# Two output projections from F32R to F16, with powers of two per channel that travel from the gated output into W_out

## The chip, the cores and the metric

The kernel runs on one core of one Trainium2 chip. The metric is the device time of one execution in microseconds (us), median over runs. The core has a matrix engine (PE, whose weight loads are listed apart as PEld), three elementwise engines (DVE, ACT, POOL) and a sequencer SP, on whose queue all DMAs of this kernel are issued. PE, DVE, ACT, POOL and SP each take their own instructions strictly in the order in which the program lists them and wait for each other through semaphores.

## The reference

Two layers over x of 1024 x 1024 f32; layer 0 mixes with forgetting attention (FoX, 16 heads of 64), layer 1 with native sparse attention (NSA, 4 groups of 4 heads).

```python
def reference(x, norm_g, fox_w_in, ..., nsa_w_out, final_g):
    for i in range(2):
        h = rmsnorm(x, norm_g[i])
        y = fox_mixer(h, ...) if i == 0 else nsa_mixer(h, ...)
        x = x + y
    return rmsnorm(x, final_g)

def fox_mixer(h, w_in, b_f, w_out):      # nsa_mixer ends in the same line
    q, k, v, f, z = split(h @ w_in)
    logits = q @ k.T * scale + c[:, None] - c[None, :]      # c: cumulated log-sigmoid of f
    o = softmax(causal(logits)) @ v
    return (o * silu(z)) @ w_out
```

What the change touches is the last line of both mixers: the gated output o*silu(z), 1024 tokens by 1024 channels, times W_out, 1024 by 1024.

## The kernel before

**Accuracy.** The results must be those of f32. A product A·B is made as three matmuls of half-precision-like parts, hi·hi + hi·lo + lo·hi (`mm3`, whose three lines are L225, L226 and L227; so every product in the profile shows those three lines). Parts are either F32R (an f32 tile rounded for the fast f32 path) or F16. The out-projections use F32R; layer 1's input projections use F16.

**Stages.** The span of 1461 us runs through: the opening (norm of x, transposes, first weights) to about 75 us; the body of FoX from there to about 510; the end of FoX with the first part of layer 0's out-projection to about 600, and the rest of that projection (`out_rest0`) to 639; NSA's projections and its compressed branch to about 957; NSA's selected and window attention to about 1387; and the rest of layer 1's out-projection (`out_rest`) with the final norm to the end.

**What sets the order.** Work is written as generators that yield their cost. `merge` takes a main generator (attention: `fox_main`, later NSA's) and a filler (`fox_fill`: the projections k, v, q, z of the next pairs of heads and then `out_start0`; in NSA `nsa_zs`: the z projections and then `out_start`) and emits so much filler per unit of main work. What comes out is one fixed order for each engine. So a matmul of the filler that waits holds up the attention's matmuls behind it, and the other way round.

**Pairs.** Heads come in pairs p = 0 to 7, a pair being 128 channels. `FoxDuo.finish` writes a pair's attention output into a tile `o` (L748; one buffer, used by one pair after the other), transposes it per half s of the tokens (s = 1, then 0), multiplies it on DVE by `vsc` and the gate silu(z) into the z tile (L758), and sends that f32 tile to `oF` in DRAM (L759). NSA's closing step does the same with DVE (L1642), POOL (the product by the gate, L1643) and a DMA. In the softmax L709 is DVE's score-and-maximum step, L718 ACT's exponential, L719 and L720 the F16 split of the probabilities, L721 their transposing DMA; in NSA the like are L1559 to L1566 and L242/L243.

**Out-projection.** W_out is copied from DRAM to DRAM at the start of each layer's filler (`wo_copy`, 16 DMAs of 512 KB), and loaded in halves of 512 rows by `load_wout`, which splits it in chunks of 128 x 512: ACT casts hi (L653), DVE or POOL in turn subtracts lo (L654). `out_start0` and `out_start` load 128-token tiles `of` from `oF` as their channels become ready, split them on ACT (L602, L1448) and DVE (L603, L1449), multiply, and add the product to the residual on DVE (L624, L1470). Pair 7, the last, also goes through `oF`. The split of a tile is emitted one half ahead of its matmuls:

```python
                if soon:
                    (load, split)[half](n + 1)
```

**Squares.** Powers of two that scale weights come from sums of squares: `early` and `late` load weight tiles `sq` and let ACT square them (L182), one step at certain points of the filler.

Of the kernel before, what the change touches and what calls it, by code (L numbers as in the profile page):

```python
# [8 lines left out]
F32 = mybir.dt.float32  # L9
# [12 lines left out]
P = 128  # L22
# [19 lines left out]
def tile_fox_nsa(ctx, tc, a, out):  # L42
# [160 lines left out]
    def gain_scale(gB):  # L203
# [12 lines left out]
        return e, b  # L216

# [130 lines left out]
    oF = dram.tile([D, S], F32, name="oF")  # L348
# [182 lines left out]
    def fox_z(p, w, halves=(1, 0)):  # L531
        zs = ready.setdefault(("zt", p), {})
        for half in halves:
            pt = ps_a(f"z{p}_{half}")
            yield from project(w, hT, half, pt)
            zs[half] = z = sb[0].tile([P, 512], F32, tag="z", bufs=4, name=f"z_{p}_{half}")
            silu2(z, pt)
            ready["z", p, half] = zs
# [4 lines left out]
                    + [(a["nsa_w_g"].rearrange("(k p) c -> p k c", p=P), 40)], 512, 1)  # L543
    first = []

    def fox_fill():
        for p in range(8):
# [12 lines left out]
            wo_copy(0, p)  # L560
# [5 lines left out]
            else:  # L566
                wq, wz = next_w(), next_w()
                yield from fox_q(p, wq, (1,))
                yield from fox_z(p, wz, (1,))
                rows0 = load_wout(hp, 0, 1)  # L570
# [3 lines left out]
                yield from fox_z(p, wz, (0,))  # L574
                yield from out_start0(load_wout(hp, 0, 0))
# [3 lines left out]
    def out_start0(rows1):  # L579
# [11 lines left out]
        def load(n):  # L591
# [4 lines left out]
            pend[n] = wp.tile([P, KC, P], F32, tag="wst", bufs=1, name=f"of0_{t}_{k}"), *out_parts(f"0_{t}_{k}")  # L596
            dma(pend[n][0][:, k:stop, :], oF[k * P:stop * P, t * P:(t + 1) * P].rearrange("(k p) t -> p k t", p=P))

        def split(n):
            _, k, stop = parts[n]  # L600
            of, oh, ol = (x[:, k:stop, :] for x in pend[n])
            A.copy(oh, of)  # L602
            V.tensor_tensor(ol, of, f(oh), OP.subtract)  # L603
# [4 lines left out]
        split(0)  # L608
        for n, (t, k0, stop) in enumerate(parts):
# [4 lines left out]
            for half in range(2):  # L614
                if soon:
                    (load, split)[half](n + 1)
# [7 lines left out]
                V.tensor_tensor(xs0[t][:, cs], pt, xs0[t][:, cs], OP.add)  # L624
            if more and not soon:
# [15 lines left out]

    def load_wout(pool, i, half):

        hi, lo = (pool.tile([P, 4, D], F32R, tag=f"h{half}{x}", name=f"wo{i}_{half}_{x}") for x in range(2))
        for k in range(4):
            r = 4 * (1 - half) + k
            dma(f(lo[:, k, :]), wD[i][r * P:(r + 1) * P, :])
        yield 0
        for k in range(4):
            for c in range(2):  # L650
                yield 400 if i else 200
                cs = slice(c * 512, c * 512 + 512)
                A.copy(hi[:, k, cs], f(lo[:, k, cs]))  # L653
                (V if c else G).tensor_tensor(lo[:, k, cs], f(lo[:, k, cs]), f(hi[:, k, cs]), OP.subtract)  # L654
        ready.setdefault("wout", []).append((hi, lo))
# [1139 lines left out]
```

## Time and profile before

| | |
|---|---|
| median of 3 runs | 1460.49 us (1459.36 to 1460.82) |
| the profiled execution | 1463.23 us, its span 1461.4 us |
| mean granted PE clock in it | 0.985 |
| busy: PE, DVE, ACT, POOL | 94%, 75%, 60%, 38% of the span |

All numbers below are of that one profiled execution; its own time stands 2.74 us above the median. In the profile's rows a name left of "<-" is what the instruction writes, names right of it what it reads, with buffer numbers left out; "[2.83 <-DVE m L709]" says that the engine sat idle 2.83 us before that instruction and that a DVE instruction of line 709 ended the wait. A matmul's duration reaches past the start of the next one; what a matmul costs in a dense stream is the distance of two starts.

### The profile page before, as it was taken

The numbers are of one execution on the slowest core, as the hardware profiler recorded it, in microseconds if no ns is written. First come the engines' busy times: TensorE is split into PE (matmuls) and PEld (weight loads), VectorE is DVE, ScalarE is ACT, GpSimd is POOL, SyncE is SP. The second block draws the span as 40 slices with busy tenths as digits, with TensorE's granted clock in tenths as the row PEclk, the third lists the DMA queues.
The fourth block names the chain that finished last, engine by engine and source line by source line (L and its number), as shares of the span: only waits on it lengthen the run. The fifth ranks groups of instructions, "written<-read, shape, count | busy, mean of one in ns | idle before, by whom it ended". The sixth has DMA issues, their size and how long they took to land.

```text
span 1461.4 us, 30097 instructions
## 1 busy us (share of the span) xinstructions
PE 1376.6 (94%) x10491; PEld 997.5 (68%) x10491; DVE 1096.5 (75%) x2882; ACT 880.7 (60%) x2198; POOL 562.1 (38%) x753
## 2 busy tenths in 40 slices
PE   5999999999999989999999988889999989988998
PEld 4878888888888767764545544456677667666786
DVE  6586778787877788586757676878898878887844
ACT  5376667676654655255534475667777777785523
POOL 2232323332232320121203455246666756776500
PEclk9999999999999999999999999999999999999999
DMA  7888887988967898464434356464678675775344
GB/s 253 269 174 185 198 188 184 211 190 194 184 155 159 204 209 173 107 223 152 147 111 140 124 133 149 118 153 114 127 147 189 125 159 130 143 166 125 81 148 144
DMA packets 413512, 237.00 MB, mean 162 GB/s; under 512 B 334448, under 2 KB 373040, under 8 KB 413104
## 3 DMA queue, kind: packets, MB, share of 16 engines
q1 hardware_dynamic: 413360, 235.07, 66.8%
q8 instruction: 83, 1.36, 0.4%
q14 instruction: 69, 0.57, 0.1%
HBM read 121.55 MB, written 37.81 MB: 109 GB/s over the span
## 4 chain that ended last, share of the span: by engine, by line
PE 31%; DVE 11%; ACT 5%; issue 3%; DMA 2%; POOL 2%; SPq 1%; DVEq 0%; ACTq 0%; POOLq 0%
PE S_n L1551 5%; PE ptp_n L1584 3%; DVE P_n L1559 2%; ACT P_n L1562 2%; PE y L225 2%; PE y L226 2%; PE y L227 2%; PE O_n L1592 1%; PE O_n L1594 1%; ACT cP L1277 1%; PE O_n L1593 1%; DVE ptl_n L243 1%; PE nz L227 1%; PE nz L226 1%; PE nz L225 1%
## 5 line engine op out<-in xcount | busy, mean ns | idle before, releaser
L1551 PE MATMUL S_n<-nk,nq 128*128 128x320 f16 (+5 forms) x768 | 153.3, 315 | 12.1 <-DVE m_n L1559 7.6
L718 ACT ACTIVATE P<-P,m 128x512 f32<-128x512 f32 (+1 forms) x192 | 116.5, 608 | 72.0 <-DVE m L709 71.3
L689 POOL TENSOR_TENSOR Bd<-B,tri 128x128 f32<-128x128 f32 x128 | 62.0, 499 | 236.9 <-DVE m L709 228.3
L1566 POOL TENSOR_TENSOR hl_n<-P_n,hl_n 128x640 f16<-128x640 f32 (+4 forms) x128 | 141.9, 1108 | 9.8
L720 DVE SCALAR_TENSOR_TENSOR hl<-P,hl 128x512 f16<-128x512 f32 (+1 forms) x192 | 115.6, 620 | 20.4 <-ACT hl L719 19.1
L1565 POOL CAST hl_n<-P_n 128x640 f16<-128x640 f32 (+4 forms) x128 | 75.1, 587 | 124.1 <-ACT P_n L1562 97.2
L1562 ACT ACTIVATE P_n<-P_n,m_n,units 128x640 f32<-128x640 f32 (+4 forms) x128 | 100.3, 784 | 34.4 <-DVE m_n L1561 33.2
L1562 ACT ACTIVATE P_n<-P_n,m_n 128x640 f32<-128x640 f32 (+7 forms) x128 | 98.6, 770 | 24.6 <-DVE m_n L1559 23.4
L1551 PEld LDWEIGHTS <-nq 128*128 128x128 f16 x768 | 71.2, 98 | 55.9 <-issue 17.2
L242 ACT ACTIVATE pth_n<-ptp_n 128x512 f16<-128x512 f32 (+1 forms) x160 | 85.9, 545 | 35.6 <-PE ptp_n L1584 33.4
L243 DVE SCALAR_TENSOR_TENSOR ptl_n<-ptp_n,pth_n 128x512 f16<-128x512 f32 (+1 forms) x160 | 99.6, 632 | 9.0 <-ACT pth_n L242 8.1
L1584 PE MATMUL ptp_n<-ident,P_n 128*128 128x128 f32 x576 | 94.0, 282 | 4.4 <-DVE ptl_n L243 1.4
L225 PE MATMUL y<-wo,ohi 128*128 128x512 f32 x230 | 95.5, 415 | 2.4 <-DVE xr L1470 1.1
L719 ACT ACTIVATE hl<-P 128x512 f16<-128x512 f32 (+1 forms) x192 | 92.4, 513 | 2.2 <-DMA pT<-hl 0.8
L1559 DVE CUSTOM_DVE_ANT_0 P_n<-S_n,wmask 128x640 f32<-128x640 f32 (+4 forms) x128 | 83.4, 651 | 12.1 <-PE S_n L1551 11.2
L226 PE MATMUL y<-wo,ohi 128*128 128x512 f32 x230 | 91.8, 399 | 0.0
L227 PE MATMUL y<-wo,olo 128*128 128x512 f32 x230 | 91.3, 397 | 0.0
L1584 PEld LDWEIGHTS ptp_n<-ident,P_n 128*128 128x128 f32 x576 | 66.2, 142 | 27.6 <-DVE ptl_n L243 10.9
L1592 PE MATMUL O_n<-nv,pth_n 128*128 128x64 f16 x576 | 72.0, 194 | 4.2 <-ACT pth_n L242 3.9
L1559 DVE CUSTOM_DVE_ANT_0 P_n<-S_n,bias,units 128x640 f32<-128x640 f32 (+1 forms) x64 | 68.8, 1075 | 8.5 <-PE S_n L1551 8.3
L1593 PE MATMUL O_n<-nv,pth_n 128*128 128x64 f16 x576 | 71.4, 194 | 0.0
L700 PE MATMUL S<-KH,Q 128*128 128x512 f32 (+1 forms) x192 | 64.0, 349 | 7.0 <-DVE m L709 7.0
(463 smaller groups left out, 4585.2 us busy)
## 6 DMA issues: line engine op xcount, KB each, us to landing
sq<-in_nsa_w_dram SPq DMA_DIRECT2D x40, 256.0 KB
B<-cD SPq DMA_DIRECT2D x16, 512.0 KB
wo<-wD SPq DMA_DIRECT2D x16, 512.0 KB
nq<-qD SPq DMA_DIRECT2D x64, 128.0 KB
x<-in_x_dram SPq DMA_DIRECT2D x8, 512.0 KB
wst_k<-in_fox_w_dram SPq DMA_DIRECT2D x8, 512.0 KB
wst_v<-in_fox_w_dram SPq DMA_DIRECT2D x8, 512.0 KB
wD<-in_fox_w_out_dram SPq DMA_DIRECT2D x8, 512.0 KB
```

What stands on the lines that cost most here:

```text
L225: T.matmul(ps, wh, mh, start=first, stop=False, **kw)
L226: T.matmul(ps, wh, ml, start=False, stop=False, **kw)
L227: T.matmul(ps, wl, mh, start=False, stop=last, **kw)
L243: V.scalar_tensor_tensor(lo[:, 0:n], pt[:, 0:n], scale, h, OP.mult, OP.subtract)
L718: A.activation(L[:, 0:n], L[:, 0:n], AF.Exp, bias=init, scale=-1.0, accum_out=self.lr[:, col + c:col + c + 1])
L719: A.activation(hi[:, cs], L[:, 0:n], AF.Copy, scale=UP)
L720: V.scalar_tensor_tensor(lo[:, cs], L[:, 0:n], UP, hi[:, cs], OP.mult, OP.subtract)
L1551: T.matmul(ps[:, b, 0:w], self.q[x][:, qi * P:(qi + 1) * P], k[:, k0 + b * w:k0 + b * w + w], start=(x == 0), stop=(x == 1))
L1559: V.tensor_tensor_reduce(dst, src, mk, 1.0 if y else unit, 3e38, OP.add, OP.min, m)
L1562: A.activation(L, L, AF.Exp, bias=m, scale=minus if y else -1.0, accum_out=self.l[:, y, qi:qi + 1])
L1566: G.tensor_tensor(hl[:, n:2 * n], L, hl[:, 0:n], OP.subtract)
L1584: T.transpose(pt[:, (x + i) * P:(x + i + 1) * P], L[:, kb * P - k0:(kb + 1) * P - k0], ident)
```

## The change

The numbers in `oF` become F16 pairs hi and lo, one DRAM tile per layer. So that F16 holds them, the gated output of each channel is multiplied by a power of two `ready["c", p]`, drawn from the sum of squares of that channel's z and, in NSA, from `limits` on v; the row of W_out that meets the channel takes the inverse power, and the product is multiplied by one power `undo` for the whole layer when it is added to the residual. What each place does:

- `fox_z` and `nsa_z`: ACT squares each half of z out of PSUM and accumulates (16 times a layer), and after the second half of a pair DVE makes the powers in four to seven operations of width 1.
- `finish` and NSA's close: after the scaled product (in NSA a second DVE operation takes the place of POOL's), ACT casts hi, POOL subtracts lo, and the DMA goes out from that tile: in FoX in place of the pair's tile `o` itself, in NSA in place of the tile that held the attention output. Pair 7 stays in SBUF (`ready["o7"]`), without DRAM.
- `load_wout16` in place of `wo_copy` and `load_wout`: straight from the input; ACT casts with a scale per row; for the lo half DVE does one scaled subtraction, or POOL two operations (scale, subtract).
- `out_start0`, `out_rest0`, `out_start`, `out_rest`: `of` comes as F16 pairs into one of two tiles in turn; the splits are gone; the residual add is a multiply-add with `undo`. All 768 matmuls of the out-projections are F16.
- `early` and `late` get 16 and 8 more tiles (W_out's rows) to square; `out_scales` gathers the sums through two tiny matmuls.
- With pair 7, `fox_fill` now runs z's projection ahead of q's, and `nsa_zs` all of z before W_out is split.

```diff
-    oF = dram.tile([D, S], F32, name="oF")
+    oF = [dram.tile([D, NT, 2, P], F16, name=f"oF{i}") for i in range(2)]
...
     def fox_z(p, w, halves=(1, 0)):
...
             zs[half] = z = sb[0].tile([P, 512], F32, tag="z", bufs=4, name=f"z_{p}_{half}")
+            A.activation(z, pt, AF.Square, accum_out=zq[:, half:half + 1])
             silu2(z, pt)
+            if half == 0:
+                V.tensor_tensor(zq[:, 2:3], zq[:, 0:1], zq[:, 1:2], OP.add)
+                half_root(zq, 2)
+                V.tensor_scalar(zq[:, 5:6], zq[:, 4:5], 2.0 ** 46, None, OP.mult)
+                V.scalar_tensor_tensor(ao[0][:, p:p + 1], zq[:, 3:4], 2.0 ** 81, ready["v", p][1], OP.mult, OP.mult)
+                ready["c", p] = zq[:, 5:6]
...
-            wo_copy(0, p)
...
+                yield from fox_z(p, wz)
                 yield from fox_q(p, wq, (1,))
-                yield from fox_z(p, wz, (1,))
+                ready["wscale"], ready["undo"] = out_scales(ao[0], sums[:, 49:65], "o0", un0, sb[0])
-                rows0 = load_wout(hp, 0, 1)
+                rows0 = load_wout16(hp, "fox_w_out", 1, 200)
                 yield next(rows0)
                 yield from fox_q(p, wq, (0,))
                 yield from rows0
-                yield from fox_z(p, wz, (0,))
...
-            pend[n] = wp.tile([P, KC, P], F32, tag="wst", bufs=1, name=f"of0_{t}_{k}"), *out_parts(f"0_{t}_{k}")
+            pend[n] = out_tile(n, f"0_{t}_{k}")
...
-                if soon:
-                    (load, split)[half](n + 1)
+                if soon and half == 0:
+                    load(n + 1)
...
-                V.tensor_tensor(xs0[t][:, cs], pt, xs0[t][:, cs], OP.add)
+                V.scalar_tensor_tensor(xs0[t][:, cs], pt, ready["undo"], xs0[t][:, cs], OP.mult, OP.add)
...
+    def load_wout16(pool, src, half, pace, scale=None):
+        lo = pool.tile([P, 4, D], F32, tag=f"h{half}1", name=f"wos_{src}_{half}")
         for k in range(4):
             r = 4 * (1 - half) + k
+            dma(lo[:, k, :], a[src][r * P:(r + 1) * P, :])
         yield 0
+        w = pool.tile([P, 2, 4, D], F16, tag=f"h{half}0", name=f"wo_{src}_{half}")
         for k in range(4):
+            r = 4 * (1 - half) + k
+            sc = ready["wscale"][:, r:r + 1]
             for c in range(2):
+                yield pace
                 cs = slice(c * 512, c * 512 + 512)
+                A.activation(w[:, 0, k, cs], lo[:, k, cs], AF.Copy, scale=sc)
+                if c:
+                    V.scalar_tensor_tensor(w[:, 1, k, cs], lo[:, k, cs], sc, w[:, 0, k, cs], OP.mult, OP.subtract)
+                else:
+                    G.tensor_scalar(lo[:, k, cs], lo[:, k, cs], sc, 1.0, OP.mult, OP.mult)
+                    G.tensor_tensor(w[:, 1, k, cs], lo[:, k, cs], w[:, 0, k, cs], OP.subtract)
+
+    def out_tile(n, name):
+        t = wp.tile([P, KC, 2, P], F16, tag=("whi", "wlo")[n % 2], bufs=2, name=f"of{name}")
+        return t, t[:, :, 0], t[:, :, 1]
...
-                    V.scalar_tensor_tensor(z, pt, ready["v", p][1], z, OP.mult, OP.mult)
-                    dma(oF[p * P:(p + 1) * P, s * 512:(s + 1) * 512], z)
+                    V.scalar_tensor_tensor(z, pt, ready["c", p], z, OP.mult, OP.mult)
+                    if p == 7:
+                        ot = ready["o7"][:, 4 * s:4 * s + 4]
+                    else:
+                        ot = o[:, 4 * s:4 * s + 4].bitcast(F16).rearrange("p t (x q) -> p t x q", x=2)
+                    z4 = z.rearrange("p (t q) -> p t q", t=4)
+                    A.copy(ot[:, :, 0], z4)
+                    G.tensor_tensor(ot[:, :, 1], z4, ot[:, :, 0], OP.subtract)
+                    if p < 6:
+                        early.step(z[:, 0:1])
+                    if p < 7:
+                        dma(oF[0][p * P:(p + 1) * P, 4 * s:4 * s + 4], ot)
...
-            G.tensor_tensor(o, o, ready["z", p, s][s], OP.mult)
-            dma(oF[p * P:(p + 1) * P, s * 512:(s + 1) * 512], o)
+            V.scalar_tensor_tensor(o, o, ready["c", p], ready["z", p, s][s], OP.mult, OP.mult)
...
+            A.copy(ot[:, :, 0], o4)
+            G.tensor_tensor(ot[:, :, 1], o4, ot[:, :, 0], OP.subtract)
+            if p < 7:
+                dma(oF[1][p * P:(p + 1) * P, 4 * s:4 * s + 4], ot)
```

Three places of the order, each as its engine's queue of instructions; "[waits ...]" names the semaphores that an instruction waits for (an engine's, or one of the DMA queue's eight, DMAHW).

DVE in FoX, where pair 1 begins to write the tile `o` that pair 0 has just left. Before:

```order
L746 TENSOR_REDUCE ot_0_0_1761<-O_0_0_1705 128x128 [waits PE_49]
L720 SCALAR_TENSOR_TENSOR hl_0_2_1656<-P_0_2_0_0_1682,hl_0_2_1656 128x512 [waits Activation_49]
L131 CAST whi_q_1742<-wst_q_1740 128x1024 [waits DMAHW7_49,PE_49]
L432 TENSOR_TENSOR KL_0_1583<-k_1_1639,KH_0_1581 64x512 [waits Activation_49]
L748 TENSOR_TENSOR o_1758<-ot_0_0_1761,l_0_0_1400 128x2x64 [waits DVE_49]
L709 ISA P_0_3_1_0_1771,m_0_3_1_1769<-S_0_3_1_0_1770,Bd_0_3_1_1767 128x128 [waits PE_49,Pool_49]
L709 ISA m_0_3_1_1769 128x1
```

After, the same stretch, whose softmax step is now L746 and whose write of `o` is now L785:

```order
L783 TENSOR_REDUCE ot_0_0_1790<-O_0_0_1734 128x128 [waits PE_49]
L757 SCALAR_TENSOR_TENSOR hl_0_2_1685<-P_0_2_0_0_1711,hl_0_2_1685 128x512 [waits Activation_49]
L131 CAST whi_q_1771<-wst_q_1769 128x1024 [waits DMAHW7_49,PE_49]
L463 TENSOR_TENSOR KL_0_1598<-k_1_1661,KH_0_1596 64x512 [waits Activation_49]
L785 TENSOR_TENSOR o_1787<-ot_0_0_1790,l_0_0_1408 128x2x64 [waits DMAHW0_49,DMAHW1_49,DVE_49,Pool_49]
L746 ISA P_0_3_1_0_1800,m_0_3_1_1798<-S_0_3_1_0_1799,Bd_0_3_1_1796 128x128 [waits PE_49]
L746 ISA m_0_3_1_1798 128x1
```

The order is the same. The write of `o` (L748, now L785) waited only for DVE's own results; now it also waits for two DMAs, pair 0's transfers out of the same tile, and for POOL, which wrote it last.

ACT in NSA attention, in the softmax of block n8 (`pth_n` is the F16 hi part of transposed probabilities, `P_n` the exponentials). Before:

```order
L242 ACTIVATE pth_n_1_2_15505<-ptp_n_1_2_15500 128x512 [waits PE_49,Activation_49]
L1562 ACTIVATE P_n_0_1_1_15550,l_n_0_15451<-P_n_0_1_1_15550,m_n_0_1_1_15551,units 128x256 [waits DVE_49,Activation_49,Pool_49]
L1562 ACTIVATE P_n_0_0_2_15586,l_n_0_15451<-P_n_0_0_2_15586,m_n_0_0_2_15587 128x384 [waits DVE_49]
L1448 CAST ohi_4_0_18254<-of_4_0_18253 128x512 [waits DMAHW3_49]
L242 ACTIVATE pth_n_1_3_15545<-ptp_n_1_3_15540 128x512 [waits PE_49]
L1562 ACTIVATE P_n_0_1_2_15614,l_n_0_15451<-P_n_0_1_2_15614,m_n_0_1_2_15615,units 128x384 [waits DVE_49,Activation_49,Pool_49]
L242 ACTIVATE pth_n_1_4_15581<-ptp_n_1_4_15576 128x512 [waits PE_49,Activation_49]
L242 ACTIVATE pth_n_1_5_15609<-ptp_n_1_5_15604 128x512 [waits PE_49,Activation_49]
```

After:

```order
L273 ACTIVATE pth_n_1_2_15769<-ptp_n_1_2_15764 128x512 [waits PE_49]
L1625 ACTIVATE P_n_0_0_3_15914,l_n_0_15714<-P_n_0_0_3_15914,m_n_0_0_3_15915 128x512 [waits DVE_49]
L273 ACTIVATE pth_n_1_3_15811<-ptp_n_1_3_15806 128x512 [waits PE_49]
L1625 ACTIVATE P_n_0_1_2_15880,l_n_0_15714<-P_n_0_1_2_15880,m_n_0_1_2_15881,units 128x384 [waits DVE_49,Activation_49,Pool_49]
L1712 CAST ot_n_0_15175<-no_0_14651 128x4x128 [waits DMAHW3_49,DVE_49,Pool_49]
L273 ACTIVATE pth_n_1_4_15847<-ptp_n_1_4_15842 128x512 [waits PE_49,Activation_49]
L273 ACTIVATE pth_n_1_5_15875<-ptp_n_1_5_15870 128x512 [waits PE_49,Activation_49]
L1625 ACTIVATE P_n_0_1_3_15948,l_n_0_15714<-P_n_0_1_3_15948,m_n_0_1_3_15949,units 128x512 [waits DVE_49,Pool_49]
```

The cast of `of` (L1448), which waits for a DMA, is gone from between the softmax's steps; a cast of pair 3's gated output (L1712), which waits for DVE, stands nearby instead.

POOL at the end of FoX, where the first half of W_out is split between the masks `Bd` that POOL makes for the scores. Before:

```order
L689 TENSOR_TENSOR Bd_1_2_0_6312<-B_1_6104,tri 128x128 [waits DVE_49]
L654 TENSOR_TENSOR wo_1_1_6155<-wo_1_1_6155,wo_1_0_6154 128x512 [waits DMAHW7_49,PE_49,Activation_49]
L689 TENSOR_TENSOR Bd_1_3_1_6381<-B_1_6104,tri 128x128 [waits DVE_49]
L689 TENSOR_TENSOR Bd_1_3_0_6393<-B_1_6104,tri 128x128 [waits DVE_49]
L654 TENSOR_TENSOR wo_1_1_6155<-wo_1_1_6155,wo_1_0_6154 128x512 [waits DMAHW1_49,Activation_49]
L654 TENSOR_TENSOR wo_1_1_6155<-wo_1_1_6155,wo_1_0_6154 128x512 [waits DMAHW3_49,Activation_49]
L654 TENSOR_TENSOR wo_1_1_6155<-wo_1_1_6155,wo_1_0_6154 128x512 [waits DMAHW4_49,Activation_49]
L689 TENSOR_TENSOR Bd_0_0_1_6479<-B_0_6474,tri 128x128 [waits DMAHW5_49,DVE_49]
L689 TENSOR_TENSOR Bd_0_0_0_6492<-B_0_6474,tri 128x128 [waits DVE_49]
```

After:

```order
L726 TENSOR_TENSOR Bd_1_3_0_6579<-B_1_6256,tri 128x128 [waits DVE_49]
L726 TENSOR_TENSOR Bd_0_0_1_6660<-B_0_6655,tri 128x128 [waits DMAHW6_49,DVE_49]
L686 TENSOR_SCALAR wos_fox_w_out_6448<-wos_fox_w_out_6448,un_359 128x512 [waits DMAHW4_49,PE_49,Activation_49]
L687 TENSOR_TENSOR wo_fox_w_out_6545<-wos_fox_w_out_6448,wo_fox_w_out_6545 128x512 [waits PE_49,Pool_49]
L726 TENSOR_TENSOR Bd_0_0_0_6673<-B_0_6655,tri 128x128 [waits DVE_49]
L686 TENSOR_SCALAR wos_fox_w_out_6448<-wos_fox_w_out_6448,un_359 128x512 [waits DMAHW5_49,Activation_49]
L687 TENSOR_TENSOR wo_fox_w_out_6545<-wos_fox_w_out_6448,wo_fox_w_out_6545 128x512 [waits Pool_49]
L726 TENSOR_TENSOR Bd_0_1_1_6749<-B_0_6655,tri 128x128 [waits DVE_49]
L686 TENSOR_SCALAR wos_fox_w_out_6448<-wos_fox_w_out_6448,un_359 128x512 [waits DMAHW7_49,Activation_49]
L687 TENSOR_TENSOR wo_fox_w_out_6545<-wos_fox_w_out_6448,wo_fox_w_out_6545 128x512 [waits Pool_49]
L726 TENSOR_TENSOR Bd_0_1_0_6762<-B_0_6655,tri 128x128 [waits DVE_49]
```

Each chunk that falls to POOL is now two instructions in the place of one, and the chunks come one mask (here block pair 0's first) later in the queue.

More of the change, by code (lines that the diff above doesn't have):

```diff
@@ L157, in split_w16 @@
         return hi, lo
-    sums = consts.tile([P, 49], F32, name="sums")
+    sums = consts.tile([P, 65], F32, name="sums")
     class Squares:
@@ L165, in __init__ @@
             self.pool, self.items, self.size, self.bufs, self.at = pool, items, size, bufs, []
+            self.out = sums
         def load(self):
@@ L532, in fox_z @@
         zs = ready.setdefault(("zt", p), {})
+        if not ao:
+            ao.append(sb[0].tile([P, 8], F32, name="ao0", bufs=1))
+        zq = sb[0].tile([P, 6], F32, tag="zq", bufs=3, name=f"zq_{p}")
         for half in halves:
@@ L573, in fox_fill @@
                 yield from rows0
-                yield from fox_z(p, wz, (0,))
-                yield from out_start0(load_wout(hp, 0, 0))
+                ready["o7"] = hp.tile([P, NT, 2, P], F16, tag="h11", name="o7_0")
+                yield from out_start0(load_wout16(hp, "fox_w_out", 0, 200))
     xs0 = {}
@@ L963, in tile_fox_nsa @@
     last = []
-    late = Squares(pa, [(a["nsa_w"][i], 29 + i) for i in range(12, 20)], D, 2)
+    late = Squares(pa, [(a["nsa_w"][i], 29 + i) for i in range(12, 20)] + row_sets(a["nsa_w_out"], D, 0), D, 2)
+    late.out = pers.tile([P, 8], F32, name="sums1")
+    ao1 = pers.tile([P, 8], F32, name="ao1")
     late.load()
@@ L1398, in nsa_zs @@
             yield from nsa_z(p, zw[p])
-        wo_copy(1, 7)
-        yield lambda: ("done", 5) in ready
-        w = zw[7]
-        yield from nsa_z(7, w, (1,))
-        rows0 = load_wout(h1, 1, 1)
-        yield next(rows0)
-        yield from nsa_z(7, w, (0,))
+        assert not late.items and not late.at
+        ready["wscale"], ready["undo"] = out_scales(ao1, late.out, "o1", pers.tile([P, 12], F32, name="un1"), pers)
         yield from rows0
-        yield from out_start(load_wout(h1, 1, 0))
+        ready["o7"] = h1.tile([P, NT, 2, P], F16, tag="h11", name="o7_1")
+        yield from out_start(load_wout16(h1, "nsa_w_out", 0, 400))
     class Halves:
@@ L1463, in out_start @@
             for half in range(2):
-                if soon:
-                    (load, split)[half](n + 1)
+                if soon and half == 0:
+                    load(n + 1)
                 _, oh, ol = pend[n]
@@ L1469, in out_start @@
                 if t in xs1:
-                    V.tensor_tensor(xs1[t][:, cols2[half]], pt, xs1[t][:, cols2[half]], OP.add)
+                    V.scalar_tensor_tensor(xs1[t][:, cols2[half]], pt, ready["undo"], xs1[t][:, cols2[half]], OP.mult, OP.add)
             if more and not soon:
@@ L1657, in out_rest @@
         dma(gB, a["final_g"].to_broadcast([P, D]))
[L1658 to L1664 removed]
+        o7, un = ready["o7"], ready["undo"]
         for t in (4, 5, 6, 7, 0, 1, 2, 3):
@@ L1679, in out_rest @@
                 if t in (1, 2, 3):
-                    for _ in products(pt, w, oh, ol, half, range(KC), True):
+                    for _ in products(pt, w, oh, ol, half, range(7), False):
                         pass
-                else:
-                    wh, wl = w[1]
-                    mm3(pt, lh[:, t, :], ll[:, t, :], wh[:, 3, cs], wl[:, 3, cs], t not in ys1, True)
-                V.tensor_tensor(xt[:, cs], pt, xt[:, cs], OP.add)
+                wh, wl = w[1]
+                mm3(pt, o7[:, t, 0], o7[:, t, 1], wh[:, 3, cs], wl[:, 3, cs], t in (4, 5, 6), True)
+                V.scalar_tensor_tensor(xt[:, cs], pt, un, xt[:, cs], OP.mult, OP.add)
                 nm.square(cs)
```

142 lines of the change are left out of this document (79 added, 63 removed).

## The prediction

> **What bounds the kernel now.** I read the page's busy times first, then the busy times by stage, then the matrix engine's waits where a stage shows it idle.
>
> ```profile
> span 1461.4 us, 30097 instructions
> ...
> PE 1376.6 (94%) x10491; PEld 997.5 (68%) x10491; DVE 1096.5 (75%) x2882; ACT 880.7 (60%) x2198; POOL 562.1 (38%) x753
> ```
>
> PE is the engine to watch, yet an average over stages hides where. Each row below is one stretch: its bounds, its length, busy us of PE, PEld, DVE, ACT and POOL, then the granted clock.
>
> ```profile
> 90.00:480.00 390.00, 390.00 (x2450) 317.98 (x2449) 299.04 (x929) 254.43 (x667) 126.50 (x201) 1.00 0.84 185
> 957.00:1387.00 430.00, 405.34 (x5038) 291.47 (x5038) 363.67 (x967) 312.74 (x713) 277.77 (x328) 0.99 0.65 138
> 1170.00:1200.00 30.00, 26.39 (x311) 18.92 (x309) 22.27 (x59) 19.65 (x45) 16.18 (x19) 0.89 0.67 152
> 1290.00:1320.00 30.00, 23.50 (x301) 16.68 (x300) 25.00 (x64) 22.56 (x52) 25.06 (x27) 0.98 0.76 170
> ```
>
> In FoX's body PE never rests (390 of 390), and DVE is busy 77% of it. In NSA attention PE rests 25 us of 430 while DVE is at 85%: there the softmax engines set some of the pace. The worst stretch is 1290 to 1320, where POOL has 25.06 of 30. The out-projection's own share, by the same columns with only the tile `y` counted:
>
> ```profile
> 510.00:540.00 30.00, 18.57 (x73) 13.22 (x73) 3.41 (x5) 1.00 1.04 229
> 540.00:570.00 30.00, 22.98 (x89) 15.94 (x89) 6.06 (x9) 1.00 0.68 153
> 570.00:600.00 30.00, 19.40 (x75) 14.16 (x74) 3.44 (x5) 0.94 0.64 152
> 600.00:645.00 45.00, 37.08 (x152) 27.82 (x150) 11.97 (x19) 0.98 0.46 157
> 1320.00:1387.00 67.00, 30.30 (x95) 15.92 (x96) 5.48 (x8) 0.98 0.45 100
> 1387.00:1461.00 74.00, 67.57 (x291) 54.19 (x289) 13.58 (x20) 0.99 0.43 144
> ```
>
> 443 of the matmuls (152 + 291) stand in two stretches in which nothing but them runs on PE. The other 325 of 768 lie among attention.
>
> **The change, part by part.** *The rate of a matmul.* Two dense streams of 512 columns: the end of the y stream (F32R, shown as f32) and an F16 stream with the same shapes.
>
> ```profile
> 1451.63 0.39 PE L225 MATMUL y<-wo,ohi 128*128 128x512 f32 x1
> ...
> 1454.18 0.39 PE L227 MATMUL y<-wo,olo 128*128 128x512 f32 x1
> ...
> 652.35 0.38 PE L225 MATMUL pn_kc<-hT,whi_nkc 128*128 128x512 f16 x1
> ...
> 655.81 0.38 PE L226 MATMUL pn_kc<-hT,whi_nkc 128*128 128x512 f16 x1
> ```
>
> The first pair is 11 starts apart, 2.55 us or 0.2318 us each; the second 16 starts, 3.46 us or 0.2163 us each. A matmul that goes from F32R to F16 should save 0.0155 us. On the 443 that run alone this is 6.9 us and lies on the path whole. On the other 325 it is 5.0 us, and only as far as PE is what ends there; I take two thirds, 3.4. Term: -10.3, between -6.9 and -11.9.
>
> By the Trainium skill ("TensorE: Matmul & The Clock Gate", section "Back-to-back issue gap") a warm matmul costs its columns over 2.4 GHz plus 2.5 ns, 216 ns for 512 columns, and the operand type does not enter. The F16 stream agrees (216.3 ns); the F32R stream does not (231.8 ns). By the page alone this term would be zero and the forecast some 10 us higher.
>
> *The splits of `of`.* The costliest stands inside the softmax of NSA: ACT reaches the cast of the first tile 0.2 us after its load was issued, and the attention waits behind it.
>
> ```profile
> L1443 SPq DMA_DIRECT2D of<-oF x2: 373/398/424, 1175.4 to 1181.3; - x2
> ...
> 1178.95 0.62 ACT L1448 CAST ohi<-of 128x512 fp32r<-128x512 f32 x1 [3.69 <-DMA of<-oF]
> ...
> 1176.38 0.19 PE L1594 MATMUL O_n<-nv,ptl_n 128*128 128x64 f16 x1
> 1180.12 0.24 PE L1592 MATMUL O_n<-nv,pth_n 128*128 128x64 f16 x1 [3.54 <-ACT pth_n L242]
> ...
> 1182.99 0.61 PE L225 MATMUL nz<-hT,zw 128*128 128x512 f16 x1
> 1183.40 0.63 PE L226 MATMUL nz<-hT,zw 128*128 128x512 f16 x1
> ```
>
> PE loses 3.54 us, and then runs slow: 0.41 us between the last two starts in place of 0.216, and 0.89 mean clock in that stretch above, which is 3.3 us of 30. The change has no cast there, and reads `of` only in matmuls that come much later, when W_out is split. What is late next in that place is the softmax chain itself on DVE and ACT, so I take -4 of these 6.8, ends 0 and -6.8. The new ACT cast in this stretch waits for DVE and not for a DMA.
>
> *The end of FoX.* Here the load of W_out and its splits hold the scores.
>
> ```profile
> 500.20 1.14 ACT L653 CAST wo<-wo 128x512 fp32r<-128x512 f32 x2 [6.54 <-DMA wo<-wD]
> ...
> 501.37 1.34 DVE L654 TENSOR_TENSOR wo<-wo,wo 128x512 fp32r<-128x512 f32 x1 [5.13 <-ACT wo L653]
> ...
> 503.43 0.80 PE L700 MATMUL S<-KH,Q 128*128 128x512 f32 x1 [2.83 <-DVE m L709]
> ```
>
> The DMA is issued at the same dependency after the change (the tile it fills is freed by pair 7's projections), so ACT's 6.5 us wait may stay, now behind z's projection moved ahead. Gone are eleven casts of `of` on ACT, twelve on DVE with pair 7's, and ACT's DMA waits with them. New is a chain: POOL takes two operations a chunk.
>
> ```profile
> L654 POOL TENSOR_TENSOR wo<-wo,wo x16: 1257/1272/1798, 500.9 to 1320.3; 128x512 fp32r<-128x512 f32 x16
> ...
> L151 POOL TENSOR_SCALAR wst_nv<-wst_nv,roots_late x16: 473/478/910, 810.5 to 853.4; 128x256 f32<-128x256 f32 x16
> ...
> L1185 POOL TENSOR_TENSOR nvs<-nvT,nvs x8: 1153/1160/1167, 858.7 to 898.9; 128x512 f16<-128x512 f32 x8
> ```
>
> The scaling of 512 columns is about twice 0.478, say 0.95; with 1.16 for the F16 subtract a chunk takes 2.1 us in place of 1.27. Four chunks of the first half with the masks between are about 10 us, against 24 matmuls of q (5.6 us) and the scores that PE has ahead of the first y. So the first y may wait up to 5 us. Term: -2, between -6 (of the waits that vanish) and +5.
>
> *The tile `o`, seven times in FoX's body.* Before, its readers were PE's transposes. Now the next pair's first write waits for cast, subtract and DMA.
>
> ```profile
> 152.37 0.73 DVE L758 SCALAR_TENSOR_TENSOR z<-pto,vsc,z 128x512 f32<-128x512 f32 x1
> ...
> 160.66 0.50 DVE L748 TENSOR_TENSOR o<-ot,l 128x128 f32<-128x128 f32 x1
> ```
>
> From the end of the product (153.10) to the write (160.66) are 7.6 us. Into them go now ACT's cast (0.6, as the cast of `of` above), POOL's subtract (1.16), the issue on SP (0.4) and the DMA: 3.5 us by the `of` row above, so 5.7 us with nothing in the queues. It fits with 1.9 us to spare; each queue (ACT behind exponentials, SP behind transposes and other transfers) can eat that. If DVE stalls, its in-order queue holds the next softmax maxima, and PE the scores behind them. I take +2 for seven pairs; ends 0 and +14 (2 us each). The transfers on SP wait for POOL, with copies of k and transposes of probabilities queued behind them; that is in the same ends.
>
> *NSA attention.* Removed: eight DVE splits of `of` and 16 POOL products. Added on DVE: 16 products, and about seven tiny operations for each of eight pairs.
>
> ```profile
> L1642 DVE SCALAR_TENSOR_TENSOR no<-ptn_n,vinv,no x16: 734/740/750, 1015.3 to 1386.3; 128x512 f32<-128x512 f32 x16
> ...
> L1449 DVE TENSOR_TENSOR olo<-of,ohi x8: 548/692/1532, 1179.6 to 1398.2; 128x512 fp32r<-128x512 f32 x3, 128x384 fp32r<-128x384 f32 x3, 128x896 fp32r<-128x896 f32 x2
> ...
> 157.63 0.16 DVE L743 TENSOR_TENSOR l<-l 128x1 f32<-128x1 f32 x1 [1.03 <-ACT P L718]
> ```
>
> 16 x 0.74 + 56 x 0.16 - 8 x 0.69 = +15 us on DVE, from 85% to 88% of the stage. ACT gains 16 casts and 16 squares, 16 x (0.6 + 0.7), at 73% busy. PE does not wait for either most of the time; I take a fifth of DVE's, +3, ends 0 and +15. POOL: 16 subtracts for 16 products is even, but its eight chunks of W_out gain 0.85 us each, 7 us in and around the stretch where it has 25.06 of 30. The transposes of the probabilities wait for POOL there. Take +2.5, ends 0 and +7.
>
> A rule of the Trainium skill speaks against this part: POOL shares its SBUF interfaces with DVE, which contends when DVE has two SBUF inputs ("GPSIMD Engine Reference", section "8. Key points"). The row of L654 shows it can be so, median 1272 ns and longest 1798. By that worst case on each of the eight chunks it would add some 4 us more; the median says that it is rare.
>
> *What costs nothing.* Sixteen squares of z and sixteen more of W_out in FoX's body: some 32 us of ACT in 390 where it has 136 idle. The copies of W_out: 16 DMAs fewer in the opening, where no row of PE's waits names them, and eight more loads later. The multiply-add with `undo` costs DVE a few hundredths of a us each. The roots of the sums hide behind q's matmuls; if that cover is gone they are 14 operations of 0.16, 2 us, which is within the end of FoX's +5. The first NSA weights may load earlier, since their staging tile no longer holds `of`: -1, ends 0 and -3.
>
> Sum: -10.3 - 4 - 2 + 2 + 3 + 2.5 - 1 = -9.8. Against the profiled execution's 1463.2 this is 1453.4; that execution stands 2.7 over the median, so the median to expect is 1450.7.
>
> **The rivals.**
>
> *The tile `o` decides (slower).* Its price is the time by which DVE is late, seven times, plus what PE runs slow after a pause as it did at 1183. For it: the single buffer and 1.9 us to spare on a path through four queues. Against: DVE is busy 77% there and PE has projections to run. The other terms sum to -11.8, so it ends on the slower side from 11.8 / 7 = 1.7 us a pair, and at 2.5 us a pair (17.5) the time is 1466.
>
> *DVE becomes the bound of NSA attention.* All 15 us and POOL's 7 show: +16.5 over my terms, 1467; half of it, 1459, no change to measure. For it: 85% busy and PE idle 25 us. Against: the waits of PE in that stage sum to less than 25 us and some are DMA and ACT.
>
> *F16 is no faster.* The page's rule above: the F32R rate would be the place's, not the type's, say the way both operands change there. Then the first term is 0 and the time 1461, no change. Against: both streams are dense, with a weight load for each matmul.
>
> *All waits go.* The end of FoX gives its 6, 1176 its 6.8, the rate its 11.9, the weights their 1, and nothing comes back: 1460.5 - 25.7 = 1435, or with my three costs (7.5) 1442. For it: these waits are rows; against: what is freed usually meets the next wait.
>
> **How the numbers follow.** The forecast (1446 to 1456): 0.60. All waits go (1436 to 1446): 0.10. F16 no faster: 0.05. DVE the bound: 0.12, of which half within 0.2%. The tile `o`: 0.13, of which 0.03 only lessens the gain. About 0.2%, 2.9 us, is what a measurement here tells from no change. Faster: 0.60 + 0.10 + 0.03 = 0.73. Same: 0.05 + 0.06 = 0.11. Slower: 0.06 + 0.10 = 0.16. The range from 1438 to 1463 leaves out the extremes of the first and the last rival.
>
> **What would show it.** Right: y's starts 0.216 us apart in the two lone stretches, y's end of layer 0 about 2.4 us and the last stretch about 4.5 us shorter; no 3.5 us gap of PE near 1176; DVE's idle ahead of the write of `o` under 0.5 us each. Wrong: a row that has that write waiting for POOL or for the DMA of `oF` by microseconds; PE below 390 of 390 in FoX's body; a y that waits for `wo` on POOL at 515; PE idle in 1290 to 1320 grown from 6.5 us; the late y matmuls waiting for `of` themselves.

## The result: 1.1% slower, and the profile after

| | before | after |
|---|---|---|
| median | 1459.97 us (1459.36 to 1460.82, 4 runs) | 1476.68 us (1475.47 to 1477.65, 4 runs) |
| ratio to before | | 1.0112, 95% interval 1.01 to 1.0125 |
| profiled execution | 1463.23 us, span 1461.4 us | 1477.65 us, span 1475.8 us |

The forecast was 1450.7 us with a range of 1438 to 1463 us. Single executions further down stood far out (3475.86 us in e1, whose median without it is 1460.13 us; 1644.49 us of the kernel before, beside e5 to e8; 1470.98 us in e9), and the ratios leave out the first two. The page of the changed kernel:

```profile
span 1475.8 us, 30392 instructions
...
PE 1371.1 (93%) x10499; PEld 931.0 (63%) x10499; DVE 1112.8 (75%) x3010; ACT 924.5 (63%) x2344; POOL 594.2 (40%) x785
```

PE is busy 5.5 us less and the span is 14.4 us longer: the time is in pauses. (In the changed kernel the three lines of `mm3` are L256 to L258, the square is L183, the F16 split of the probabilities L756 and L757.) To see where, I counted the same matmuls in both traces and compared their starts (the scores `S` of FoX and `S_n` of NSA, and the out-projection's `y`). The last column is the first experiment, below. Each column is one traced execution.

| start of | before | after | difference | e1 minus before |
|---|---|---|---|---|
| S of FoX, 153rd pair of 192 | 474.3 | 494.7 | +20.4 | +1.1 |
| first y of layer 0 | 515.1 | 533.5 | +18.4 | +3.0 |
| last y of layer 0 | 638.9 | 652.9 | +14.0 | -2.8 |
| first S_n of NSA | 959.5 | 971.5 | +12.0 | -5.8 |
| 65th S_n | 990.1 | 1008.8 | +18.7 | +0.8 |
| 417th S_n | 1168.5 | 1191.1 | +22.6 | +5.2 |
| 449th S_n | 1193.7 | 1210.6 | +17.0 | -0.6 |
| last S_n | 1374.2 | 1396.0 | +21.8 | +2.4 |
| last y of layer 1 | 1454.2 | 1468.5 | +14.3 | -5.0 |

So: 20 us lost in FoX's body, 6 won at its end, 2 in NSA's projections, 7 lost at the start of NSA attention, 6 won between the 417th and the 449th score, 9 lost in the rest of NSA attention, 7.5 won in the last stretch.

**FoX's body.** The stretch that had 390.00 of 390 before:

```profile
90.00:480.00 390.00, 377.53 (x2330) 304.34 (x2329) 288.46 (x921) 269.43 (x722) 127.69 (x199) 0.99 0.85 189
```

The loss comes in steps: the starts of the scores fall behind by 4.2 us between 218 and 231 us of the kernel before and by 4.7 us between 431 and 438, and the rest in smaller steps. The first of these two, engine by engine (ACT, SP, DVE, PE; the number in brackets is the idle time ahead):

```profile
215.64 0.62 ACT L801 CAST o<-z 128x512 f16<-128x512 f32 x1
216.16 0.20 ACT L182 ACTIVATE zg<-z 128x1 f32<-128x1 f32 x1
220.51 0.72 ACT L183 ACTIVATE sq<-sq,zg 128x512 f32<-128x512 f32 x1 [4.15 <-DMA sq<-in_nsa_w_dram]
...
221.35 0.58 ACT L462 CAST KH<-k 64x512 fp32r<-64x512 f32 x1
...
216.13 1.06 SPq L173 DMA_DIRECT2D sq<-in_nsa_w_dram  x1
...
221.96 0.69 DVE L463 TENSOR_TENSOR KL<-k,KH 64x512 fp32r<-64x512 f32 x1 [5.51 <-ACT KH L462]
...
233.26 0.22 PE L771 MATMUL O<-v,pT 128*128 128x128 f16 x1 [2.49 <-ACT zg L182]
```

`finish` now calls a step of `early`. The square tile has one buffer, and its next load can be issued only when the last square has read it: SP issues it at 216.13, and ACT comes to the step from `finish` 0.03 us later. So ACT waits 4.15 us at the head of its own queue, with the cast of k behind it, DVE waits for that cast, and PE stands 2.49 us at 233.26. Over the stretch, the waits of ACT for square tiles, of the kernel before and then after:

```profile
ACT sq L182 <- DMA sq<-in_nsa_w_dram: 8.0, 7, 2.1
...
ACT sq L183 <- DMA sq<-in_nsa_w_dram: 24.8, 14, 4.3
ACT sq L183 <- DMA sq<-in_fox_w_out_dram: 10.7, 7, 2.8
ACT sq L183 <- DMA sq<-in_nsa_w_g_dram: 2.9, 1, 2.9
```

38.4 us in place of 8.0. DVE's waits for ACT in the same stretch, before:

```profile
DVE hl L720 <- ACT hl L719: 14.9, 25, 1.4
DVE KL L432 <- ACT KH L431: 8.2, 10, 3.4
```

and after, with the one wait ahead of a write of `o`:

```profile
DVE hl L757 <- ACT hl L756: 36.1, 31, 4.5
...
DVE KL L463 <- ACT KH L462: 18.2, 10, 6.6
...
DVE o L785 <- DMA oF<-o: 1.2, 1, 1.2
```

The last row is the rival that I had priced at seven times 2 us: the write of the tile `o` waited once, 1.2 us.

**The start of NSA attention.** ACT, DVE and PE at the first softmax:

```profile
978.33 0.60 ACT L1450 ACTIVATE nz<-nz 128x512 f32<-128x512 f32 x1 [1.92 <-PE nz L258]
...
979.05 0.16 DVE L1453 TENSOR_TENSOR nzq<-nzq 128x1 f32<-128x1 f32 x1 [6.12 <-ACT nz L1450]
...
981.12 2.10 PE L1614 MATMUL S_n<-nk,nq 128*128 128x384 f16 x8 [2.82 <-DVE m_n L1622]
```

An addition of one column, the first step of a pair's power, stands at the head of DVE's queue 6.12 us because the square that it sums waits on ACT for a z that PE has not finished; the first maxima queue behind it.

**What came as forecast.** The end of layer 1's y stream is 24 starts in 5.18 us from the first to the last of these rows, 0.216 us each:

```profile
1463.33 0.38 PE L258 MATMUL y<-wo_nsa_w_out,o 128*128 128x512 f16 x1
...
1468.51 0.38 PE L258 MATMUL y<-wo_nsa_w_out,o 128*128 128x512 f16 x1
```

And PE's wait of 3.5 us near 1176 is gone. The groups of PE's `O_n` matmuls in both pages, before and after (last number: idle time ahead of the group):

```profile
L1592 PE MATMUL O_n<-nv,pth_n 128*128 128x64 f16 x576 | 72.0, 194 | 4.2 <-ACT pth_n L242 3.9
...
L1655 PE MATMUL O_n<-nv,pth_n 128*128 128x64 f16 x576 | 71.7, 193 | 0.2
```

### The profile page after: what moved, and what is told of

Same layout as the page of the kernel before. It is cut to its first block, busy times and chain, and to the rows that moved or that the text cites. A ratio compares the mean times of both kernels' runs of the same rounds, so it can differ in the third digit from the quotient of the medians.

```text
span 1475.8 us, 30392 instructions
## 1 busy us (share of the span) xinstructions
PE 1371.1 (93%) x10499; PEld 931.0 (63%) x10499; DVE 1112.8 (75%) x3010; ACT 924.5 (63%) x2344; POOL 594.2 (40%) x785
## 5 line engine op out<-in xcount | busy, mean ns | idle before, releaser
L1614 PE MATMUL S_n<-nk,nq 128*128 128x320 f16 (+5 forms) x768 | 156.8, 318 | 17.4 <-DVE m_n L1622 16.1
L757 DVE SCALAR_TENSOR_TENSOR hl<-P,hl 128x512 f16<-128x512 f32 (+1 forms) x192 | 115.3, 616 | 41.2 <-ACT hl L756 39.9
L756 ACT ACTIVATE hl<-P 128x512 f16<-128x512 f32 (+1 forms) x192 | 92.6, 512 | 2.0 <-ACT P L755 0.4
L183 ACT ACTIVATE sq<-sq,zg 128x512 f32<-128x512 f32 (+2 forms) x73 | 59.5, 815 | 39.7 <-DMA sq<-in_nsa_w_dram 24.8
L771 PE MATMUL O<-v,pT 128*128 128x128 f16 x576 | 59.4, 223 | 13.7 <-DMA pT<-hl 9.8
L1657 PE MATMUL O_n<-nv,ptl_n 128*128 128x64 f16 x576 | 68.8, 193 | 0.3 <-DVE ptl_n L274 0.3
```

Source lines behind the costliest of these rows:

```text
L756: A.activation(hi[:, cs], L[:, 0:n], AF.Copy, scale=UP)
L757: V.scalar_tensor_tensor(lo[:, cs], L[:, 0:n], UP, hi[:, cs], OP.mult, OP.subtract)
L1614: T.matmul(ps[:, b, 0:w], self.q[x][:, qi * P:(qi + 1) * P], k[:, k0 + b * w:k0 + b * w + w], start=(x == 0), stop=(x == 1))
```

## The experiments

The theory after this reading (S): the added square steps hold ACT, not by their work but by their place. Its rival (O): the tile `o`. For NSA: the place of the tiny operations (N), against the load on DVE (L, D). "Ratio" is to the kernel before, measured beside each, with its 95% interval. Apart from the three executions named above, those of e1 to e10, and of the kernel before beside them, scatter by some 4 us around the medians, so the intervals decide. The kernel before has 1459.88 us beside e1 to e4, 1460.56 beside e5 to e8 and 1459.34 beside e9 and e10. A trace is one execution and scatters too: e1, e4 and e6 issue the same instructions up to the first S_n, and it starts at 953.7, 956.4 and 959.8 us. The length of a stage says more than the place of its start.

**e1.** Drop the step in `finish`, load the first tile ahead so that the projections' steps get through all 57.

```diff
-                    if p < 6:
-                        early.step(z[:, 0:1])
...
                 sb.append(tc.alloc_tile_pool(name="sb", bufs=2, reuse_waits="tile"))
+                early.load()
```

> The changed kernel, with all its squares, but without the twelve square steps in the finish of pairs 0 to 5; the first tile is loaded ahead instead, so that the steps of the projections alone get through all 57 tiles. Theory S: in the body of FoX ACT's in-order queue waits for the single square tile's DMA, because a finish step follows a step of k's projection closer than a DMA takes, with the casts of k and the exponentials of the softmax behind it (38 us of such waits against 8 before). Then the body loses most of its 20 us: 8 to 14 us faster than the changed kernel, 1463 to 1469 us, and ACT's waits for square DMAs fall below 20 us. Rival O: the next pair's write of the tile o waits for cast, subtract and DMA; untouched here, so the time stays at 1474 to 1479 us.

Measured: 1460.44 us, ratio 1.0007 (0.999 to 1.0024). FoX's body is back, with the handling of the tile `o` untouched:

```profile
90.00:480.00 390.00, 388.16 (x2422) 315.18 (x2420) 300.30 (x951) 273.99 (x725) 134.68 (x207) 1.00 0.87 192
...
ACT sq L183 <- DMA sq<-in_fox_w_out_dram: 8.8, 3, 5.9
ACT sq L183 <- DMA sq<-in_nsa_w_dram: 8.5, 6, 2.4
```

ACT's busy time is even 4.6 us higher than in the changed kernel's same stretch, and its waits for squares are 17.3 us. Fifty square steps stand in this stretch, against 55 in the changed kernel and 39 before, and PE sees next to nothing of them: the place counts and not the work. S is confirmed, though the gain of 16.2 us is above the 8 to 14 that I expected; O falls. What this does not separate is ACT's queue from SP's. Ahead of the loads of square tiles SP stood at the head of its own queue for 40.7 us after the change, 17.9 before and 24.3 in e1 (rows of SP's waits, summed), with other transfers behind them, and two of PE's pauses in the changed kernel, 4.2 of its 12.5 idle us, end with a transposing DMA of probabilities. The edit takes away both.

**e2.** As e1, with no squares of W_out in FoX at all.

```diff
-                    + [(a["nsa_w_g"]..., 40)] + row_sets(a["fox_w_out"], 512, 49), 512, 1)
+                    + [(a["nsa_w_g"]..., 40)], 512, 1)
+    V.memset(sums[:, 49:65], 0.5)
```

> As e1, and the sixteen tiles of layer 0's W_out are not loaded nor squared in FoX at all: a constant of about their size stands in their place (left out of the computation). This prices all of the added squares of FoX. Theory S: a little below e1, 10 to 18 us faster than the changed kernel, 1459 to 1467 us; the body of FoX is within 4 us of the kernel before. Rival O: 1474 to 1479 us as e1, with at most 2 us from ACT's lighter load.

Measured: 1454.79 us, ratio 0.9962 (0.9948 to 0.9976). The first y starts 3.5 us earlier than in e1. What the loads and squares of W_out still cost in e1 lies at the end of FoX: from the 153rd pair of S to the first y it is 37.7 us here and 42.6 in e1. In e1 the last square stands at 512.9 and the scales wait for it; that this wait is the cost is not shown, and e7 and e9 speak against it.

**e3.** The changed kernel, with the powers of an NSA pair tied to the next pair's z.

```diff
             if half == 0:
-                V.tensor_tensor(zq[:, 2:3], zq[:, 0:1], zq[:, 1:2], OP.add)
...
+                def power(after=None, p=p, zq=zq, zs=zs):
+                    if after is not None:
+                        V.scalar_tensor_tensor(zq[:, 0:1], after[:, 0:1], 0.0, zq[:, 0:1], OP.mult, OP.add)
...
+                powers.append(power)
...
+            if half == 1 and powers:
+                powers.pop(0)(z)
```

> The changed kernel with the eight tiny operations that make a pair's powers in NSA tied to the next pair's z, so that they stand later in DVE's queue. Theory N: at 979 us such an operation stands at the head of DVE's in-order queue 6.1 us, waiting for ACT's square of a z that PE has just finished, and the first softmax of NSA attention waits behind it; moved later, that gap of PE (2.8 us and the slow clock after it) goes and the whole is 3 to 6 us faster: 1471 to 1474 us. Rival L: it is the load that counts (DVE at 87% of the stage), not the place; then 1476 to 1478 us, since one operation a pair is added.

Measured: 1471.03 us, ratio 1.0091 (1.007 to 1.0112): 5.6 us below the changed kernel, the size that N gave, but the two intervals overlap and the trace does not bear the size out. The first 32 score matmuls now take 14.8 us from the first to the 33rd start, against 18.1 after and 12.9 before: the pause is as N says, and 3.3 us are won there. From the 417th to the 449th start, though, 2.2 us are lost again (21.7 against 19.5), and from the first to the last S_n the stage takes 423.5 us against 424.5. The first S_n itself starts 5.9 us earlier than in the changed kernel, where up to there both issue the same instructions. So the time in N's range is luck; the move as a whole won about 1 us.

**e4.** e1 and e3 together.

> e1 and e3 together. If the two causes are separate they add: 11 to 20 us faster than the changed kernel, 1457 to 1466 us, which would be about the kernel before. If something else bounds the whole, less than the larger of the two.

Measured: 1462.89 us, ratio 1.0026 (1.0014 to 1.0038). The two do not add: 13.8 us, less than e1's 16.2 alone. The pause at the start is gone (14.8 us for those 32), but a new one stands at a later pair; here PE, then the group of DVE that it waits for, then POOL in the same stretch:

```profile
1193.50 0.81 PE L1622 MATMUL S_n<-nk,nq 128*128 128x384 f16 x4 [2.02 <-DVE m_n L1630]
...
1188.26 0.69 DVE L86 SCALAR_TENSOR_TENSOR nz<-nz,nz 128x512 f32<-128x512 f32 x1 [0.87 <-ACT nz L85]
1188.98 1.10 DVE L1458 SCALAR_TENSOR_TENSOR nzq<-nz,nzq 128x1 f32<-128x1 f32 x1
1190.11 0.52 DVE L1459 TENSOR_TENSOR nzq<-nzq 128x1 f32<-128x1 f32 x1
...
1191.23 0.63 DVE L1462 TENSOR_TENSOR nzq<-nzq,limits 128x1 f32<-128x1 f32 x1
...
1192.57 0.88 DVE L1630 CUSTOM_DVE_ANT_0 P_n<-S_n,bias,units 128x640 f32<-128x640 f32 x1
...
1188.91 1.16 POOL L1721 TENSOR_TENSOR ot_n<-no,ot_n 128x512 f16<-128x512 f32 x1
1190.01 0.61 POOL L1636 CAST hl_n<-P_n 128x512 f16<-128x512 f32 x1
1190.70 1.15 POOL L1637 TENSOR_TENSOR hl_n<-P_n,hl_n 128x512 f16<-128x512 f32 x1
```

The chain stands in one block ahead of a maximum, 3 us from 1188.98. A one-column operation took 0.16 us at 979.05 above, and three take 0.52 to 1.10 here: those that read two tensor operands. Each of them ends 0.01 to 0.02 us after the POOL operation that was running when it began (1190.08 after 1190.07, 1190.63 after 1190.62, 1191.86 after 1191.85).

**e5.** e1 without the making of powers in NSA.

```diff
-            limits()
+            V.memset(one1, 2.0 ** -6); V.memset(ao1, 2.0 ** 6)
...
-            A.activation(z, pt, AF.Square, accum_out=zq[:, half:half + 1])
...
-                V.tensor_tensor(zq[:, 2:3], zq[:, 0:1], zq[:, 1:2], OP.add)
...
-                ready["c", p] = zq[:, 6:7]
+                ready["c", p] = ready["one"]
```

> e1, and in NSA the sixteen squares of z on ACT, the tiny operations on DVE and the limits on v are left out; constants stand in their place. It prices the making of the powers in NSA, place and load together. Theory N+L: in e1 the first 32 score matmuls of NSA attention lose 5.2 us against the kernel before, and the stage 5 more up to 1170 us; without the powers at least half of both comes back: 4 to 9 us faster than e1, 1451 to 1456 us. Rival D: the second product on DVE in place of POOL's and the added cast make the loss; then at most 3 us.

Measured: 1452.1 us, ratio 0.9943 (0.9922 to 0.9964), 8.3 us below e1 by the medians. From the first to the last score matmul of NSA attention: 410.9 us, against 422.9 in e1, 424.5 after and 414.7 before. The stage is 12.0 us shorter than in e1; in this trace its start stands 5.1 us later, 2.9 of them already at the first y, up to where the two kernels issue the same on PE. With the second product on DVE and the added casts still in, the stage is shorter than before: rival D falls, the making of the powers is the cost.

**e6.** e1 with only the powers of pairs 0 and 1 tied to the next pair's z.

```diff
-                powers.append(power)
+                if p < 2:
+                    powers.append(power)
+                else:
+                    power()
```

> e1 with the powers of pairs 0 and 1 alone tied to the next pair's z. In e4 the wait at the head of DVE's queue at the start of NSA attention was gone (the stage's first 32 score matmuls 2.0 us late in place of 5.2), but a new wait came at 1191 us. If the moved powers of the later pairs made that new wait, this keeps the gain without the loss: 2 to 5 us faster than e1, 1455 to 1459 us. If the pause was only shifted, it stays within 1.5 us of e1.

Measured: 1456.3 us, ratio 0.9978 (0.9962 to 0.9993), 4 us below e1 by the medians. It is the one kernel with the whole computation whose interval lies below 1. Its interval and e1's overlap a little, but the traces show the gain where it was sought: from the first to the last S_n 418.1 us against 422.9 in e1 (3.2 of these 4.8 in the first 32 scores), and 418.1 and 417.2 again in e9 and e10, which have the same powers. That its profiled execution itself ended 1.4 us later than e1's comes from ahead of the stage, whose start stood 6.1 us later after the same instructions.

**e7.** e1 with W_out's squares before the last seven of NSA's, and NSA's roots drawn after W_out's load.

```diff
+    early.items[34:34] = row_sets(a["fox_w_out"], 512, 49)
...
                 yield next(rows0)
+                first.append(roots(sums[:, 0:41], ..., "early"))
```

> e1 with the same 57 square tiles in another order: W_out's sixteen come before the last seven of NSA's, so that they are done a pair earlier, and the roots of NSA's weights are drawn after W_out's load is issued. In e1 PE waits 2.2 us at 511 for the sums (ACT's last squares), and the first y starts 3.0 us later than before; e2, without those squares, started it 0.5 us earlier than before. Expected: 2 to 4 us faster than e1, 1456 to 1459 us. If the wait is for the scores and not for the sums: no change to e1.

Measured: 1461.84 us, ratio 1.0017 (1.0003 to 1.0031): no gain in place of 2 to 4 us. PE waits in the same place for the other sum:

```profile
515.74 0.18 PE L196 MATMUL total_early<-sb_early,ones 128*128 128x41 bf16 x1 [2.19 <-ACT sb_early L194]
```

**e8.** e1 with all lo parts of layer 0's W_out on DVE.

```diff
-                if c:
+                if c or src == "fox_w_out":
```

> e1 with all lo parts of layer 0's W_out made on DVE (one operation each, 0.75 us) in place of half of them on POOL in two (2.1 us). In e1 the first y matmuls wait three times for POOL's chain, 4.8 us in all (518 to 526 us). Expected: these waits go, 2 to 4 us faster than e1, 1456 to 1459 us. Rival: DVE, with six microseconds more work among the last scores, delays the maxima by as much; then no change or 1 to 2 us slower.

Measured: 1460.15 us, ratio 0.9995 (0.9981 to 1.001), as e1. In e1 these waits stood there:

```profile
520.13 0.38 PE L257 MATMUL y<-wo_fox_w_out,of 128*128 128x512 f16 x1 [0.85 <-POOL wo_fox_w_out L688]
...
523.22 0.38 PE L257 MATMUL y<-wo_fox_w_out,of 128*128 128x512 f16 x1 [1.21 <-POOL wo_fox_w_out L688]
...
525.91 0.38 PE L257 MATMUL y<-wo_fox_w_out,of 128*128 128x512 f16 x1 [1.48 <-POOL wo_fox_w_out L688]
```

and in e8 none of them, but this one a little later, as the rival had it:

```profile
532.71 0.50 PE L738 MATMUL S<-KH,Q 128*128 128x512 f32 x1 [2.97 <-DVE m L747]
```

**e9.** e6, W_out's squares as in e7, but NSA's roots only after pair 7's q.

```diff
                 yield from rows0
+                first.append(roots(sums[:, 0:41], ..., "early"))
```

> e6 with W_out's squares a pair earlier as in e7, but with the roots of NSA's weights drawn only after pair 7's q, so that their tiny matmul no longer stands on PE where e7 waited for it (2.6 us at 513). If e7's gain was taken by that wait: 2 to 3 us faster than e6, 1453 to 1455 us. If what the first y waits for is POOL's chain and the scores: within 1.5 us of e6, 1455 to 1458 us.

Measured: 1456.78 us, ratio 0.9995 (0.9976 to 1.0015): within 1.5 us of e6, the second of the two outcomes expected. The matmul that gathers the sums of W_out stands at 506.8 in place of e6's 515.6, and the first y at 518.7 in place of 520.0.

**e10.** e9, with the part of the scales that depends on W_out alone drawn ahead of the last z.

```diff
                 wq, wz = next_w(), next_w()
+                w0 = roots(sums[:, 49:65], ((0, 16),), "o0w", sb[0])
...
+                w1 = roots(late.out, ((0, 8),), "o1w", pers)
                 rows0 = load_wout16(h1, "nsa_w_out", 1, 400)
```

> e9 with the part of each layer's scales that depends on W_out alone drawn before the last z projections, so that the chain of tiny operations after the last z is half as long (in e1 it stands at the head of DVE's queue around 1300 to 1312, where PE waits six times for maxima or for the scales, some 7 us). Expected 1 to 3 us faster than e9. If the waits there come from the dense softmax work and not from the chain: no change.

Measured: 1456.79 us, ratio 0.9988 (0.9977 to 1.0). The expected 1 to 3 us did not come. Neither e9 nor e10 gains on e6: what waits at the end of FoX and after the last z is not the sums alone.

## Why the prediction was wrong, point by point

*"What costs nothing"* is the step that failed. It weighed the squares by busy time ("some 32 us of ACT in 390 where it has 136 idle") and did not look at their place in the queues. Each new step is also a DMA into a tile with one buffer and a wait at the head of ACT's in-order queue. Measured: 30 us more of such waits, 20 us on the end of FoX's body; taking away the steps in `finish` alone brings 16.2 us. The steps also hold up SP's queue, and the share of each queue stays open.

*The tile `o`.* The right place, the wrong mechanism. The path of 5.7 us fitted into the 7.6 us, as the sum said: one wait of 1.2 us. The forecast's slower rival had the size and the seven steps, but in e1, with the tile handled as in the changed kernel, the body's 20.4 us shrink to 1.1, so the tile alone costs no more than that.

*NSA attention* was mis-sized as a load. The term was +3 for a fifth of DVE's 15 us. It is the making of the powers that costs: 8.3 us by e5, of which the first pause is a wait at the head of DVE's queue and not work; by place alone e6 won 4.8 us of the stage. The tiny operations were also under-counted: eight a pair in place of seven, and 13.9 us of DVE in all in place of 56 x 0.16 = 9.0, since those that read two tensor operands end only after a POOL operation that is running. The second product on DVE, the larger part of those 15 us, is mostly hidden: without the powers the stage is 3.8 us shorter than before, where the vanished splits alone won 5.6.

*POOL*, +2.5: the waits of PE that POOL ended between 955 and 1400 us are 6.2 us after and 2.1 before, so some 4 us, within its ends. The subtract of a chunk took 1.16 us in the median, 1.72 at the longest: the worst case was rare, as the forecast said.

*The splits of `of`*, -4: measured between the 417th and the 449th score, 22.6 - 17.0 = 5.6 us won, and e1 shows 5.8. Right, within its ends. One reading behind it was off: ACT stood at that cast from 1175.26, 0.14 us ahead of the load's issue at 1175.40 and not 0.2 us behind it; the sum does not change.

*The rate*, 0.0155 us a matmul: 0.216 after against 0.2318 before; right. The last stretch is 7.5 us shorter, more than the 4.5 forecast, because 303 y matmuls were left after the last score in place of 315. The rival by which the type does not matter falls. By the Trainium skill ("TensorE: Matmul & The Clock Gate", section "Back-to-back issue gap") the gap goes by the columns alone; the traces agree with its 216 ns for F16 (0.216 us) and not for F32R (0.2318 us).

*The end of FoX*, -2: from the first S past the body to the last y of layer 0 it won 20.4 - 14.0 = 6.4 us after, and 1.1 + 2.8 = 3.9 in e1. But that stretch also holds layer 0's y, whose own saving is up to 384 x 0.0155 = 6.0 us; so the end of FoX itself won next to nothing, or lost some 2 us in e1, within its ends. POOL's chain did hold the first y matmuls, 3.5 us in e1 where the forecast allowed 5; e8 shows that this wait hides another of the same size.

*The sum.* With e1 the kernel is at 1460.44 us: the forecast's 1450.7 missed even without the squares' place by some 10 us, of which e5 accounts for 8.3 (the term allowed 3) and e2 for 5.6 (the term was nil). Both leave work out together with its waits, so this is no proof that a kernel with all the work can reach 1450.

What stays open: what PE lost in FoX's body beyond its idle 12.5 us and 3.4 us of clock, out of 20.4 (after two of its pauses the granted clock was 0.51 from 234.0 to 237.5 us and 0.50 from 452.5 to 455.9); which of ACT's and SP's queues cost it; what e2 won at the end of FoX, since earlier sums alone did not win it; and which share of e5's 8.3 us is the chain at the end (from the last z to the split of W_out) and which the pairs in between.

## What to carry to other kernels

An added instruction on an engine with idle time is free only if what it waits for is there when it reaches the head of the queue: for each added operation look up its last input (a DMA into a single buffer, a sum that another engine still makes) and what is queued behind it. Give a prefetched stream steps that are further apart than one load takes; a second buffer is the other way, not tried here. One-column operations count by place, not by their 0.16 us. Judge a fix by the stage that it changes: e3's time fell as expected, but not in that stage.

## What the runs showed of the hardware

The same 512-column matmul starts every 0.2318 us in F32R and every 0.216 us in F16, in streams that are otherwise alike. Tiny DVE operations on one column wait for POOL when they read two tensor operands. In the changed kernel's powers of NSA, ten of the 16 such operations began while a POOL operation ran; nine of these took 0.30 to 1.26 us and ended 0.01 to 0.02 us after POOL's, and for the tenth POOL was done within 0.11 us. The six that met no running POOL operation took 0.16 us. The 48 that read one took 0.14 to 0.16 us, also the 21 that began while POOL ran. A 256 KB load of a square tile took 4.4 us from its issue at 216.13 to the square that read it at 220.51.
